# A two-layer hybrid decoder trunk in fp32: q and k by the two-part product, the rotary swap by transfers, the head norm's Newton steps on GpSimd, and attention stages at other distances

## The chip, the cores and the metric

The kernel runs on one core of one Trainium2 chip, in one launch. The core has TensorE (PE in the profile: matrix products and transposes, with PEld for the loading of its stationary operand), VectorE (DVE), ScalarE (ACT), GpSimd (POOL) and SyncE (SP, which here only issues transfers), a scratchpad (SBUF) of 128 partitions, and PSUM, whose 8 banks of 128 x 512 fp32 take PE's results. The metric is the device time in microseconds (us) of one execution; a time shown is the median of several runs.

## The reference

The input x is 256 tokens of width 1024, in fp32. Each of two layers runs a SwiGLU block, a mixer and another SwiGLU block, each followed by a layer norm of `ALPHA*x` plus the block's output. The change lies in the mixer's branch B, differential attention with 8 heads, each with two score maps of dimension 64 and values of width 128:

```
def _mixer(x, ...):
    z = x @ w_in
    u, v, q, k, val, gates = jnp.split(z, SPLITS, axis=-1)
    ...
    q = _rope(q.reshape(bsz, seq, N_DIFF_HEADS, 2, DIFF_HEAD_DIM), cos, sin)
    k = _rope(k.reshape(bsz, seq, N_DIFF_HEADS, 2, DIFF_HEAD_DIM), cos, sin)
    ...
    o = _diff_attention(q, k, val, lam_full)
    o = _rmsnorm(o, diff_ln_g) * (1.0 - lam_init)
    ...
    m = g[:, :, 0] * (h_a @ w_branch[0]) + g[:, :, 1] * (h_b @ w_branch[1])
    return m @ w_out

def _rope(x, cos, sin):
    x1, x2 = jnp.split(xf, 2, axis=-1)
    out = jnp.concatenate([x1 * c - x2 * s, x2 * c + x1 * s], axis=-1)

def _diff_attention(q, k, v, lam):
        s = jnp.where(mask, s, neg)
        p = jax.nn.softmax(s, axis=-1)
        a = p[:, :, 0] - lam * p[:, :, 1]
        return jnp.einsum('bhqk,bkhe->bqhe', a.astype(v.dtype), v)

def _rmsnorm(x, g):
    y = xf * lax.rsqrt(jnp.mean(jnp.square(xf), axis=-1, keepdims=True) + LN_EPS)
```

The mixer's projection `w_in` gives seven sections of width 1024: u, v, q, k, val and two gates.

## The kernel before

**Products in parts.** A matrix product in fp32 is made of three products of a shorter type, fp32r. Each operand is cut into a high part (a copy by ACT, L166 for weights, L173 for activations) and a low part (the difference, a subtraction by DVE, L168 and L174); high times high, low times high and high times low are summed in PSUM. The activations x lie with both parts side by side: `both(k)` (L87) is a 128 x 512 view of the k-th slice of x, the high part of 256 tokens in its first half and the low part in its second; `xh(k)` and `xl(k)` are the halves alone.

**Weights.** They stream from memory in chunks of 1 MB (128 x 2048 fp32). `stream` (L147) issues the load on SP's queue into one of 4 raw buffers, and cuts the chunk in two halves of 1024 columns, each into one of 8 `whi` and 8 `wlo` buffers, so each chunk costs ACT two copies and DVE two subtractions. A weight buffer comes free when PE has used it.

**Two forms of the product that has weights stationary and tokens moving.** One chunk of `pairs` layout holds two blocks of 128 output columns. `gemm_a` (L202, used for q and k) gives both blocks one bank: for each block and each of the 8 slices of x it runs three matmuls with 256 moving columns (`three` with `moving_x`, L200): weight-high with x-high, weight-high with x-low, weight-low with x-high. `gemm_a2` (L212, used for the gates, u, the branch products and the SwiGLU's first products) uses a bank for each block: 8 matmuls of weight-high with 512 moving columns, both parts of x at once (L219), for the two blocks, and then 8 of weight-low with the 256 high columns (L225) for each. What x-low gave lies in the bank's second half. ACT copies it out into `r` (L226), and DVE adds it to the first half into `z` (L227). The buffers `r` come from a pool of four, `s512`, shared with the attention's `pp`.

**Who sets the order.** PE's order is the order of the program, written out by hand: `tc.manual_schedule` covers PE alone. The order of ACT, DVE, POOL and SP is set by the scheduler of the framework, by priorities (`step`, L105, raises the priority number with each chunk) and its own estimate of when things are ready; `issue_after` (`behind`, L143) holds an instruction behind another one. Small pieces of work run between pieces of large products as tasks: a generator that is put beside the products, with a delay, and continued whenever a clock has come far enough. The clock is counted in beats: `gemm_a` beats 1 for each half of a product (L209), `gemm_a2` beats 0.65 for each high half and 0.35 for each low half (L220, L228), so that a product is 2 beats in either form. A `yield n` in a task sets its next piece n beats later.

**The mixer** (L500) runs in this order on PE: the values (`gemm_b2`, L511), the q and k products of four head pairs (L614 to L617), eight in each layer, then eight gate products (L624), v, u with the spatial gating, the branch products and the output product. After each pair's q and k products the attention of that pair is put beside the products that follow, so that it runs during the q and k products of the next pairs and the gate products.

**Rotary** (`rope`, L515). A product's bank holds in each of its 128 partitions one of a head's 128 features (two maps of 64), and in its columns the 256 tokens of each of two heads, the blocks; the two halves of a map's 64 features lie 32 partitions apart. Four copies by ACT (L520), of 32 partitions each, bring the halves into `swap` in exchanged places and scale them; DVE multiplies the bank by the cosine and the scale into `qk` (L524), POOL multiplies `swap` by the signed sine (L526), DVE adds (L527). `swap` comes from a pool of two buffers of 128 x 512 (`t512`, L94), which is shared with the gates' `gz`, the branches' `bz` and the SwiGLU's `silu`.

**Attention of one pair of heads** (`attend`, L530), with delay 3 and these pieces:

1. Scores of the second 128 queries against 256 keys: 4 matmuls (L544) into two side banks. DVE adds the mask and takes the negated maximum of each row (L552, four instructions), ACT takes the exponential and its row sum (L554), DVE forms the reciprocal, the factor with lambda (L558) and the combination of the two maps (L562, two instructions).
2. The same for the first 128 queries, against 128 keys.
3. Transposes of the combined probabilities by PE (L574: four, L579: two), each group copied out of PSUM by ACT (L576, L581).
4. The product with the values (L587, L589) into one side bank. ACT squares it with row sums (L595), into `on`, which is later overwritten. The head's norm is a reciprocal square root: DVE forms the sum with the epsilon (L596, L597), and `rsqrt` (L176) a first guess by integer arithmetic (L180, L181) and three Newton steps of three instructions each on 128 x 4 numbers (L189 to L191), all on DVE. The layer norms use the same function with n = 1, by another path (L186, L187). DVE multiplies the bank by the result into `on` (L599).
5. Transposes of `on` by PE (L605), and the cut in two parts (L610 on ACT, L611 on DVE) into `hb`, the branch product's operand.

PSUM is two pools of four banks: the main one for the large products, the side one for scores, transposes and value products. `gemm_a` holds one main bank for each product; `gemm_a2` holds two.

Of the kernel before, what the change touches and what calls it, by code (L numbers as in the profile page):

```python
# [19 lines left out]
P = 128  # L20
# [30 lines left out]
def trunk(ctx, tc, x, xT, w13a, w13b, w2, wb, wqk, wa, wbr, wo, gateb, sgug, sgub, sguwT, sgubias, lam, diffg,  # L51
# [22 lines left out]
    def bank():  # L74
        return psum.tile([P, 512], F32, tag="main", name=name("bank"))
# [57 lines left out]
    def beside(task, delay):  # L133
        tasks.append([clock[0] + delay, task])
# [3 lines left out]
            for task in list(tasks):  # L138
                turn(task)

    latest = [None, None]

    def behind(ins):  # L143

        return tc.issue_after(ins) if ins is not None else nullcontext()
# [30 lines left out]
    def rsqrt(v, scale, eps, n):  # L176


        ve, y = sm("ve", n), sm("yi", n, I32)
        V.tensor_scalar(out=ve, in0=v, scalar1=scale, scalar2=eps, op0=ALU.mult, op1=ALU.add)  # L180
        V.tensor_scalar(out=y, in0=ve.bitcast(I32), scalar1=-0.5, scalar2=RSQRT_START, op0=ALU.mult, op1=ALU.add)  # L181
        y = y.bitcast(F32)
        for e in (-26 / 27, -8 / 9, -2 / 3):
            a, z = sm("nwa", n), sm("nwy", n)
            if n == 1:
                V.tensor_scalar(out=a, in0=y, scalar1=y, scalar2=ve, op0=ALU.mult, op1=ALU.mult)  # L186
                V.tensor_scalar(out=z, in0=a, scalar1=3.0 * 2.0 ** e, scalar2=y, op0=ALU.subtract, op1=ALU.mult)  # L187
            else:
                V.tensor_tensor(out=a, in0=y, in1=y, op=ALU.mult)  # L189
# [5 lines left out]
    def three(ps, xh, xl, w_hi, w_lo, start, stop, moving_x):  # L195

        order = [(w_hi, xh), (w_hi, xl), (w_lo, xh)] if moving_x else [(w_hi, xh), (w_lo, xh), (w_hi, xl)]
        for n, (w, xx) in enumerate(order):
            l, r = (w, xx) if moving_x else (xx, w)
            PE.matmul(ps, l, r, start=start and n == 0, stop=stop and n == 2)  # L200

    def gemm_a(src, xh, xl):  # L202

        b = bank()
        for n, (hi, lo) in enumerate(stream(src)):
            for k in range(KT):
                s = slice(k * P, (k + 1) * P)
                three(b[:, n * T : (n + 1) * T], xh(k), xl(k), hi[:, s], lo[:, s], k == 0, k == KT - 1, True)
            beat(1)  # L209
        return b  # L210

    def gemm_a2(src, xc, z):  # L212


        b = [bank() for _ in range(2)]
        got = stream(src)
        for n, (hi, lo) in enumerate(got):
            for k in range(KT):
                PE.matmul(b[n], hi[:, k * P : (k + 1) * P], xc(k), start=k == 0, stop=False)  # L219
            beat(0.65)  # L220
        r = s512("r")
        for n, (hi, lo) in enumerate(got):
            s = slice(n * T, (n + 1) * T)
            for k in range(KT):
                PE.matmul(b[n][:, :T], lo[:, k * P : (k + 1) * P], xc(k)[:, :T], start=False, stop=k == KT - 1)  # L225
            A.activation(r[:, s], b[n][:, T:], AF.Copy)  # L226
            V.tensor_tensor(out=z[:, s], in0=b[n][:, :T], in1=r[:, s], op=ALU.add)  # L227
            beat(0.35)  # L228
        return z

    def rows_b(ps, t, k0, piece, xh, xl, kts, c0=0, n=512):

        hi, lo = piece
        for j in range(2):
            k, o = k0 + j, j * 512 + c0
            wh, wl = (w[j][:, c0 : c0 + n] if isinstance(w, list) else w[:, o : o + n] for w in (hi, lo))
            three(ps[:, :n], xh(k)[:, t * P : (t + 1) * P], xl(k)[:, t * P : (t + 1) * P], wh, wl,
                  k == 0, k == kts - 1, False)
        beat(n / 1024)

    def gemm_b(src, kts, xh, xl, done, tail=4, last=()):
# [258 lines left out]
    def mixer(l, i, norm):  # L500
# [11 lines left out]

        hb = slots("hb", 2 * KT, F32R)

        def rope(ps, scale):  # L515

            sw = t512("swap")
            for q in range(4):
                o, i = q * 32, (q ^ 1) * 32
                A.activation(sw[o : o + 32, :], ps[i : i + 32, :], AF.Copy, scale=scale)  # L520
            z = slots("qk", 2)[0]
            z3, s3 = z.rearrange("p (j t) -> p j t", j=2), sw.rearrange("p (j t) -> p j t", j=2)
# [3 lines left out]
            G.tensor_tensor(out=s3, in0=s3, in1=s, op=ALU.mult)  # L526
            V.tensor_tensor(out=z, in0=z, in1=sw, op=ALU.add)  # L527
            return z

        def attend(hp, qT, kT):  # L530
# [33 lines left out]
                return pp[0]  # L564

            second = exps(1)
            yield 1
            first = exps(0)
            yield 2
            b = side_bank()  # L570
            for j in range(2):
                for c in range(2):
# [6 lines left out]
                PE.transpose(b[:, j * P : (j + 1) * P], first[:, j * P : (j + 1) * P], ident)  # L579
# [19 lines left out]
            V.tensor_tensor(out=on.rearrange("p (q e) -> p q e", q=4), in0=b.rearrange("p (q e) -> p q e", q=4),  # L599
                             in1=r.unsqueeze(2).to_broadcast([P, 4, P]), op=ALU.mult)  # L600
            yield 3
            b = side_bank()
            for j in range(2):
                for t in range(NT):
# [186 lines left out]
```

## Time and profile before

| | |
|---|---|
| Time, median of 3 runs | 1251.56 us (1251.5 to 1252.19) |
| The profiled execution's own time | 1251.36 us |
| Its span in the trace | 1249.6 us |
| Granted TensorE clock, mean | 0.998 |
| Data moved by transfers | 237.69 MB, mean 190 GB/s |
| HBM read and written | 235.47 MB and 1.05 MB |

In the profile, the first part gives the busy time of each engine with its share of the span. The second cuts the span in 40 slices, with a digit for tenths busy:

```profile
DVE  6777567788587887765687665677886878866654
ACT  6776456897565566663466664468875555766530
POOL 0100000210000000000000000001200000000000
...
DMA  9954555445665547555547545554456654565530
```

The mixers' attention stages are where POOL has its few digits: slices 8 and 9 of layer 0, and 28 and 29 of layer 1. The list of costly groups is read as line, engine, operation, output from inputs (partitions x elements), then busy time, the mean of one in ns, and the idle time of that engine just before with what ended it:

```profile
L168 DVE TENSOR_TENSOR wlo<-raw,whi 128x1024 fp32r<-128x1024 f32 (+1 forms) x442 | 490.2, 1122 | 153.5 <-ACT whi L166 80.1
...
L219 PE MATMUL bank<-x,whi 128*128 128x512 f32 x1536 | 369.4, 392 | 0.0
...
L225 PE MATMUL bank<-x,wlo 128*128 128x256 f32 x1536 | 200.7, 284 | 0.0
```

The duration of one matmul there is its pipelined length; what it costs PE's stream is read from the chain of waits, where a number of them in sequence stand with their time together. The same chain, taken in order of time, names the line and the number of instructions of each piece of PE's work; a list of the waits of an engine names what it waited for, how long, how often, and the longest. The timeline gives single instructions or runs of one line with start and length.

### The profile page before, as it was taken

Reading aid. Unit: us, or ns where it says so; the run is one execution under the profiler, and the core shown is the slowest. Engines: PE = TensorE matmul, PEld = TensorE weight load, DVE = VectorE, ACT = ScalarE, POOL = GpSimd, SP = SyncE. Lnnn points to the kernel's source line nnn. Section 1 sums busy time; section 2 is a strip of 40 time slices with the busy share of each in tenths; the row PEclk is TensorE's granted clock in tenths of the full one; section 3 lists DMA queues with packets and bytes.
Section 4 is the critical chain, followed back from the end, with each engine's and each line's share of the span. In section 5 each row is a group of like instructions: output and inputs, shape, how many; then the busy total and the mean of one; then the engine's idle time right before and its main releaser. Section 6 shows DMA issues by size and latency. Waiting matters only on the chain.

```text
span 1249.6 us, 18211 instructions
## 1 busy us (share of the span) xinstructions
PE 1236.8 (99%) x6951; PEld 1077.1 (86%) x6951; DVE 899.9 (72%) x1637; ACT 764.1 (61%) x1365; POOL 43.8 (4%) x62
## 2 busy tenths in 40 slices
PE   9999999999999999999999999999999999999997
PEld 8888888988888888888888888899888888888886
DVE  6777567788587887765687665677886878866654
ACT  6776456897565566663466664468875555766530
POOL 0100000210000000000000000001200000000000
PEclk9999999999999999999999999999999999999999
DMA  9954555445665547555547545554456654565530
GB/s 355 318 198 175 186 182 193 175 142 185 209 215 183 187 152 249 187 186 186 201 165 241 193 163 190 196 202 136 153 185 209 216 181 169 201 235 177 180 118 34
DMA packets 37608, 237.69 MB, mean 190 GB/s; under 512 B 4321, under 2 KB 5393, under 8 KB 11409
## 3 DMA queue, kind: packets, MB, share of 16 engines
q1 hardware_dynamic: 33552, 223.89, 51.3%
q0 software_dynamic: 3536, 12.13, 2.9%
q8 instruction: 54, 0.88, 0.3%
q10 hardware_dynamic: 432, 0.52, 0.1%
q14 instruction: 34, 0.27, 0.1%
HBM read 235.47 MB, written 1.05 MB: 189 GB/s over the span
## 4 chain that ended last, share of the span: by engine, by line
PE 98%; DVE 1%; ACT 1%; issue 0%; DVEq 0%
PE bank L200 43%; PE bank L219 33%; PE bank L225 17%; PE bank L315 2%; PE sbank L544 1%; PE sbank L435 1%; PE sbank L664 1%; PE sbank L589 0%; PE sbank L327 0%; ACT swap L520 0%; PE sbank L605 0%; PE sbank L469 0%; DVE pp L562 0%; ACT pp L554 0%; PE sbank L587 0%; PE sbank L574 0%
## 5 line engine op out<-in xcount | busy, mean ns | idle before, releaser
L168 DVE TENSOR_TENSOR wlo<-raw,whi 128x1024 fp32r<-128x1024 f32 (+1 forms) x442 | 490.2, 1122 | 153.5 <-ACT whi L166 80.1
L166 ACT ACTIVATE whi<-raw 128x1024 fp32r<-128x1024 f32 (+1 forms) x442 | 425.9, 978 | 278.9 <-PE bank L200 145.6
L219 PE MATMUL bank<-x,whi 128*128 128x512 f32 x1536 | 369.4, 392 | 0.0
L219 PEld LDWEIGHTS bank<-x,whi 128*128 128x128 f32 x1536 | 282.3, 188 | 54.9
L225 PEld LDWEIGHTS bank<-x,wlo 128*128 128x128 f32 x1536 | 196.2, 191 | 7.3 <-issue 0.7
L225 PE MATMUL bank<-x,wlo 128*128 128x256 f32 x1536 | 200.7, 284 | 0.0
L200 PE MATMUL bank<-whi,hhi 128*128 128x512 f32 (+1 forms) x374 | 141.4, 378 | 0.0
L200 PE MATMUL bank<-wlo,hhi 128*128 128x512 f32 (+1 forms) x374 | 141.1, 377 | 0.0
L200 PE MATMUL bank<-whi,hlo 128*128 128x512 f32 (+1 forms) x374 | 141.0, 377 | 0.0
L226 ACT ACTIVATE r<-bank 128x256 f32<-128x256 f32 x224 | 83.3, 378 | 53.6 <-PE bank L225 53.2
L200 PE MATMUL bank<-whi,x 128*128 128x512 f32 x328 | 106.5, 394 | 0.0
L200 PE MATMUL bank<-x,whi 128*128 128x256 f32 x512 | 94.4, 286 | 0.0
L200 PEld LDWEIGHTS bank<-x,whi 128*128 128x128 f32 x512 | 79.8, 192 | 2.6 <-issue 2.0
L200 PEld LDWEIGHTS bank<-whi,hlo 128*128 128x128 f32 x374 | 70.4, 188 | 12.9
L200 PEld LDWEIGHTS bank<-wlo,hhi 128*128 128x128 f32 x374 | 70.4, 188 | 12.8
L200 PEld LDWEIGHTS bank<-whi,hhi 128*128 128x128 f32 x374 | 70.4, 188 | 12.7
L200 PE MATMUL bank<-x,wlo 128*128 128x256 f32 x256 | 72.5, 283 | 0.0
L200 PEld LDWEIGHTS bank<-whi,x 128*128 128x128 f32 x328 | 61.6, 188 | 12.5
L174 DVE TENSOR_TENSOR hlo<-silu,hhi 128x256 fp32r<-128x256 f32 x72 | 30.6, 425 | 52.5 <-ACT hhi L173 52.5
L200 PE MATMUL bank<-wlo,x 128*128 128x512 f32 x164 | 64.0, 390 | 0.0
L441 ACT ACTIVATE xf<-sbank,ln_b,ln_g 128x128 f32<-128x128 f32 x80 | 30.1, 456 | 40.1 <-PE sbank L435 40.1
L227 DVE TENSOR_TENSOR silu<-bank,r 128x256 f32<-128x256 f32 x144 | 54.3, 417 | 0.1
(166 smaller groups left out, 1348.4 us busy)
## 6 DMA issues: line engine op xcount, KB each, us to landing
raw<-in_w13a SPq DMA_DIRECT2D x72, 1024.0 KB, 5.1
raw<-in_w SPq DMA_DIRECT2D x40, 1024.0 KB, 4.8
raw<-in_wa SPq DMA_DIRECT2D x24, 1024.0 KB, 4.9
raw<-in_wb SPq DMA_DIRECT2D x16, 1024.0 KB, 5.1
raw<-in_wqk SPq DMA_DIRECT2D x16, 1024.0 KB, 5.6
raw<-in_wbr SPq DMA_DIRECT2D x16, 1024.0 KB, 5.0
raw<-in_w13b SPq DMA_DIRECT2D x12, 1024.0 KB, 5.0
raw<-in_wo SPq DMA_DIRECT2D x8, 1024.0 KB, 4.9
```

The source lines that it names most:

```text
L166: A.activation(h, r, AF.Copy)
L168: V.tensor_tensor(out=w, in0=r, in1=h.bitcast(F32), op=ALU.subtract)
L174: return a.ins, V.tensor_tensor(out=lo, in0=src, in1=hi.bitcast(F32), op=ALU.subtract).ins
L200: PE.matmul(ps, l, r, start=start and n == 0, stop=stop and n == 2)
L219: PE.matmul(b[n], hi[:, k * P : (k + 1) * P], xc(k), start=k == 0, stop=False)
L225: PE.matmul(b[n][:, :T], lo[:, k * P : (k + 1) * P], xc(k)[:, :T], start=False, stop=k == KT - 1)
L226: A.activation(r[:, s], b[n][:, T:], AF.Copy)
L227: V.tensor_tensor(out=z[:, s], in0=b[n][:, :T], in1=r[:, s], op=ALU.add)
L315: PE.matmul(ps[t][m], x[:, j, o + t * P : o + (t + 1) * P], y, start=k0 + j == 0 and o == 0 and y is hi, stop=k0 + j == KT - 1 and y is lo)
L435: PE.transpose(b[:, k * P : (k + 1) * P], self.y[t][:, h * 512 + k * P : h * 512 + (k + 1) * P], ident)
L441: A.activation(xf[:, s], b[:, s], AF.Identity, scale=self.gT[:, f], bias=self.bT[:, f])
L544: PE.matmul(banks[m][:, j * nk : (j + 1) * nk], rows(qT, m, j, t * P, P), rows(kT, m, j, 0, nk), start=True, stop=True)
```

## The change

**Products.** `gemm_a` is gone; q and k go through `gemm_a2` with the weights as before. It takes a scale (for q, 1/8; for k, 1) and the buffer for `r`, here from `t512`, the pool of two that `swap` uses too; with a scale other than 1 DVE's add becomes a multiply-add.

**Swap.** `rope` now starts from `z` in SBUF, not from the bank. Four transfers from SBUF to SBUF, issued on SP's queue, take the place of ACT's four copies. DVE multiplies `z` by the cosine in place, POOL and DVE go on as before.

**Newton steps.** For n > 1, which is the head norm alone, the three Newton steps run on POOL, each in four instructions instead of three. The guess stays on DVE.

**After the value product.** ACT first copies the bank to `on`, squares inside PSUM, and, 3.9 beats later, scales `on` in place with four instructions, each held behind the last evacuation that `gemm_a2` has put on ACT at that place of the program (`emptied`). DVE's multiply by the norm is gone.

**Stages.** The first delay goes from 3 to 3.9 beats; the distances between the pieces go from 1, 2, 3, 3 to 0.6, 2.6, 2.3, and then 3.9 to the scaling and 0.9 from there to the final transposes.

```diff
-                V.tensor_tensor(out=a, in0=y, in1=y, op=ALU.mult)
-                V.tensor_tensor(out=a, in0=a, in1=ve, op=ALU.mult)
-                V.scalar_tensor_tensor(out=z, in0=a, scalar=3.0 * 2.0 ** e, in1=y, op0=ALU.subtract, op1=ALU.mult)
+                G.tensor_tensor(out=a, in0=y, in1=y, op=ALU.mult)
+                G.tensor_tensor(out=a, in0=a, in1=ve, op=ALU.mult)
+                G.tensor_scalar(out=a, in0=a, scalar1=3.0 * 2.0 ** e, scalar2=None, op0=ALU.subtract)
+                G.tensor_tensor(out=z, in0=a, in1=y, op=ALU.mult)
...
-    def gemm_a(src, xh, xl):
...
-    def gemm_a2(src, xc, z):
+    def gemm_a2(src, xc, z, scale=1.0, r=None):
...
-        r = s512("r")
+        r = s512("r") if r is None else r
...
-            A.activation(r[:, s], b[n][:, T:], AF.Copy)
-            V.tensor_tensor(out=z[:, s], in0=b[n][:, :T], in1=r[:, s], op=ALU.add)
+            emptied[0] = A.activation(r[:, s], b[n][:, T:], AF.Copy, scale=scale).ins
+            if scale == 1.0:
+                V.tensor_tensor(out=z[:, s], in0=b[n][:, :T], in1=r[:, s], op=ALU.add)
+            else:
+                V.scalar_tensor_tensor(out=z[:, s], in0=b[n][:, :T], scalar=scale, in1=r[:, s], op0=ALU.mult,
+                                       op1=ALU.add)
...
-        def rope(ps, scale):
+        def rope(src, scale):
+            z = gemm_a2(src, both, slots("qk", 2)[0], scale, t512("r"))
             sw = t512("swap")
             for q in range(4):
                 o, i = q * 32, (q ^ 1) * 32
-                A.activation(sw[o : o + 32, :], ps[i : i + 32, :], AF.Copy, scale=scale)
-            z = slots("qk", 2)[0]
+                nc.sync.dma_start(sw[o : o + 32, :], z[i : i + 32, :])
...
-            V.scalar_tensor_tensor(out=z3, in0=ps.rearrange("p (j t) -> p j t", j=2), scalar=scale, in1=c,
-                                   op0=ALU.mult, op1=ALU.mult)
+            V.tensor_tensor(out=z3, in0=z3, in1=c, op=ALU.mult)
             G.tensor_tensor(out=s3, in0=s3, in1=s, op=ALU.mult)
             V.tensor_tensor(out=z, in0=z, in1=sw, op=ALU.add)
...
             second = exps(1)
-            yield 1
+            yield 0.6
             first = exps(0)
-            yield 2
+            yield 2.6
...
-            yield 3
+            yield 2.3
...
             on = slots("on", 2)[0]
+            A.activation(on, b, AF.Copy)
             ss, s2 = sm("ss", 4), sm("s2", 4)
             for q in range(4):
                 s = slice(q * P, (q + 1) * P)
-                A.activation(on[:, s], b[:, s], AF.Square, accum_out=ss[:, q : q + 1])
+                A.activation(b[:, s], b[:, s], AF.Square, accum_out=ss[:, q : q + 1])
...
-            V.tensor_tensor(out=on.rearrange("p (q e) -> p q e", q=4), in0=b.rearrange("p (q e) -> p q e", q=4),
-                             in1=r.unsqueeze(2).to_broadcast([P, 4, P]), op=ALU.mult)
-            yield 3
+            yield 3.9
+            for q in range(4):
+                s = slice(q * P, (q + 1) * P)
+                with behind(emptied[0]):
+                    A.activation(on[:, s], on[:, s], AF.Copy, scale=r[:, q : q + 1])
+            yield 0.9
...
         for hp in range(HEADS // 2):
-            qT = rope(gemm_a(wqk[l, hp, 0], xh, xl), HD ** -0.5)
-            kT = rope(gemm_a(wqk[l, hp, 1], xh, xl), 1.0)
-            beside(attend(hp, qT, kT), 3)
+            qT = rope(wqk[l, hp, 0], HD ** -0.5)
+            kT = rope(wqk[l, hp, 1], 1.0)
+            beside(attend(hp, qT, kT), 3.9)
```

The parameter `moving_x` of `three` goes too, since no product uses it any more.

More of the change, by code (lines that the diff above doesn't have):

```diff
@@ L139, in finish_tasks @@
                 turn(task)
-    latest = [None, None]
+    latest, emptied = [None, None], [None]
     def behind(ins):
@@ L188, in rsqrt, with three @@
             else:
-                V.tensor_tensor(out=a, in0=y, in1=y, op=ALU.mult)
-                V.tensor_tensor(out=a, in0=a, in1=ve, op=ALU.mult)
-                V.scalar_tensor_tensor(out=z, in0=a, scalar=3.0 * 2.0 ** e, in1=y, op0=ALU.subtract, op1=ALU.mult)
+                G.tensor_tensor(out=a, in0=y, in1=y, op=ALU.mult)
+                G.tensor_tensor(out=a, in0=a, in1=ve, op=ALU.mult)
+                G.tensor_scalar(out=a, in0=a, scalar1=3.0 * 2.0 ** e, scalar2=None, op0=ALU.subtract)
+                G.tensor_tensor(out=z, in0=a, in1=y, op=ALU.mult)
             y = z
         return y
[L195 to L200, printed above, removed]
-    def gemm_a(src, xh, xl):
[L204 to L210, printed above, removed]
-    def gemm_a2(src, xc, z):
+    def three(ps, xh, xl, w_hi, w_lo, start, stop):
+        for n, (w, xx) in enumerate([(w_hi, xh), (w_lo, xh), (w_hi, xl)]):
+            PE.matmul(ps, xx, w, start=start and n == 0, stop=stop and n == 2)
+    def gemm_a2(src, xc, z, scale=1.0, r=None):
         b = [bank() for _ in range(2)]
@@ L237, in rows_b @@
             three(ps[:, :n], xh(k)[:, t * P : (t + 1) * P], xl(k)[:, t * P : (t + 1) * P], wh, wl,
-                  k == 0, k == kts - 1, False)
+                  k == 0, k == kts - 1)
         beat(n / 1024)
@@ L519, in rope @@
                 o, i = q * 32, (q ^ 1) * 32
-                A.activation(sw[o : o + 32, :], ps[i : i + 32, :], AF.Copy, scale=scale)
-            z = slots("qk", 2)[0]
-            z3, s3 = z.rearrange("p (j t) -> p j t", j=2), sw.rearrange("p (j t) -> p j t", j=2)
+                nc.sync.dma_start(sw[o : o + 32, :], z[i : i + 32, :])
+            z3, s3 = (v.rearrange("p (j t) -> p j t", j=2) for v in (z, sw))
             c, s = (v.unsqueeze(1).to_broadcast([P, 2, T]) for v in (cos_t, sin_t))
-            V.scalar_tensor_tensor(out=z3, in0=ps.rearrange("p (j t) -> p j t", j=2), scalar=scale, in1=c,
-                                   op0=ALU.mult, op1=ALU.mult)
+            V.tensor_tensor(out=z3, in0=z3, in1=c, op=ALU.mult)
             G.tensor_tensor(out=s3, in0=s3, in1=s, op=ALU.mult)
```

## Prediction

> **What bounds the kernel now.** I read the page's busy shares and its chain of waits first, then the list of what TensorE (PE) waited for, then windows over the stage that the change touches.
>
> ```profile
> PE 1236.8 (99%) x6951; PEld 1077.1 (86%) x6951; DVE 899.9 (72%) x1637; ACT 764.1 (61%) x1365; POOL 43.8 (4%) x62
> ...
> PE 98%; DVE 1%; ACT 1%; issue 0%; DVEq 0%
> ```
> ```profile
> PE sbank L579 <- DVE pp L562: 1.8, 2, 0.9
> ...
> PE sbank L544 <- DVE mx L552: 0.9, 2, 0.4
> ```
> ```profile
> 211.96:322.62 110.66, 109.33 (x793) 100.16 (x791) 89.18 (x225) 90.20 (x208) 14.53 (x14) 1.00 0.52 177
> 830.06:940.72 110.66, 109.33 (x793) 100.15 (x792) 89.20 (x225) 90.20 (x208) 14.56 (x14) 1.00 0.53 177
> ```
>
> PE is the chain. Its order is written out by hand, so the time falls only if PE has less to do or waits less. Inside the kernel it waits 2.7 us in all, 0.9 + 0.4 us in each layer, on DVE. The windows run from the first q/k product to the last gate product of each layer: columns are length, busy time of PE, PEld, DVE, ACT, POOL, then clock, DMA share and GB/s. The two layers agree to 0.02 us, and DVE and ACT are 81% busy there, so a late step of either has little time to catch up. The clock is 1.00 throughout.
>
> What PE pays for each piece, from the chain in order of time:
>
> ```profile
> 55.92 3.65 PE bank L219 x16
> 59.57 1.91 PE bank L225 x16
> ...
> 224.88 7.20 PE bank L200 x60
> 232.08 1.06 PE sbank L544 x8
> ...
> 236.21 0.65 PE sbank L544 x8
> ...
> 242.81 0.44 PE sbank L574 x4
> 243.25 0.22 PE sbank L579 x2
> ...
> 254.19 0.22 PE sbank L587 x2
> ...
> 255.53 2.87 PE bank L200 x24
> ```
>
> The second stall of a layer looks like this in the timeline (GpSimd is POOL):
>
> ```profile
> 274.91 1.63 DVE L562 SCALAR_TENSOR_TENSOR pp<-pp,c,pp 128x128 f32<-128x128 f32 x2
> ...
> 275.12 1.29 POOL L526 TENSOR_TENSOR swap<-swap,sin_t 128x512 f32<-128x512 f32 x1 [9.23 <-ACT swap L520]
> ...
> 276.60 0.33 PE L579 MATMUL sbank<-ident,pp 128*128 128x128 f32 x1 [0.89 <-DVE pp L562]
> ```
>
> DVE finishes pair 2's probabilities late, and PE stands before their transposes. That is where I look for the next stall.
>
> **The change, part by part.**
>
> *Products.* A q or k product is 48 matmuls of 256 columns at 7.20/60 = 0.120 us: 5.76 us. In the other form it is 3.65 + 1.91 = 5.56 us. That is 0.20 us less for each of 16: **-3.2 us**, all on PE's chain. The same form already runs at that pace for the gates, so little is open here: bounds -2.9 and -3.2.
>
> *The old stalls.* The stages stand elsewhere, so the **-2.7 us** of waits go; whether others come is the main question below.
>
> *The swap.* Four copies on ACT go; two evacuations on ACT and one more on DVE each come. Four transfers of 64 KB on SP take their place.
>
> ```profile
> 2.19 0.91 SPq L299 DMA_DIRECT2D raw<-in_w13b  x2
> ```
> ```profile
> raw<-in_wqk SPq DMA_DIRECT2D x16, 1024.0 KB, 5.6
> ...
> out_x<-xtok SPq DMA_DIRECT2D x2, 128.0 KB, 2.0
> ```
>
> SP needs 0.45 us for each issue, 1.8 us for four. The trace has no SBUF-to-SBUF transfer; its landing is bounded below by the 2.0 us of the quiet store and above by the 5.6 us of a weight load in traffic. I take 2.5, nearer the store in size. Then: evacuations 0.8, issues 1.8, landing 2.0 to 5.6, the multiply on POOL 1.3 to 2.05, the add 0.6: 6.5 to 10.9 us after the product. The scores that need it now stand four gemm halves later, 2 x 5.56 = 11.1 us. That cover hides it; without it each late microsecond is PE's. SP now issues all eight q/k loads before the first swap, and each later load waits behind a swap, by up to one product (5.6 us). Those loads are used three products later (16.7 us) and land in 5.6: no cost. `r` and `swap` share two buffers, so the evacuation of product n waits on ACT for the add of product n-2: also 11.1 us behind it, covered likewise, and ACT's splits are what queues there.
>
> *Newton steps on GpSimd.* In the built order POOL has, in this sequence, the multiply for pair 2's k, twelve Newton steps of pair 0, then the multiply for pair 3's q. DVE has `yi` of pair 0, a split, z*cos, one evacuation, and then the add that needs that last multiply. So DVE stands at the add until Newton is through, and behind it stand the second evacuation, pair 2's row maxima and combinations, which PE's third transposes need. What it costs needs these rows:
>
> ```profile
> 211.56 5.76 DVE L168 TENSOR_TENSOR wlo<-raw,whi 128x1024 fp32r<-128x1024 f32 x5
> ...
> 222.49 0.69 DVE L527 TENSOR_TENSOR qk<-qk,swap 128x512 f32<-128x512 f32 x1 [0.69 <-POOL swap L526]
> 223.10 2.58 DVE L168 TENSOR_TENSOR wlo<-raw,whi 128x1024 fp32r<-128x1024 f32 x2
> ...
> 234.60 0.42 DVE L552 CUSTOM_DVE_ANT_0 pp<-sbank,mask 128x256 f32<-128x256 f32 x1
> ...
> 235.97 1.22 DVE L168 TENSOR_TENSOR wlo<-raw,whi 128x1024 fp32r<-128x1024 f32 x1
> ...
> 237.79 0.87 DVE L562 SCALAR_TENSOR_TENSOR pp<-pp,c,pp 128x256 f32<-128x256 f32 x2
> ...
> 256.09 0.61 DVE L562 SCALAR_TENSOR_TENSOR pp<-pp,c,pp 128x128 f32<-128x128 f32 x2
> ...
> 261.13 0.16 DVE L189 TENSOR_TENSOR nwa<-yi 128x4 f32<-128x4 f32 x1
> ...
> 262.90 0.69 DVE L599 TENSOR_TENSOR on<-sbank,nwy 128x512 f32<-128x512 f32 x1
> ...
> 263.51 1.22 DVE L168 TENSOR_TENSOR wlo<-raw,whi 128x1024 fp32r<-128x1024 f32 x1
> ...
> 263.83 2.05 POOL L526 TENSOR_TENSOR swap<-swap,sin_t 128x512 f32<-128x512 f32 x1 [5.08 <-ACT swap L520]
> ...
> 299.95 0.75 DVE L227 TENSOR_TENSOR gz<-bank,r 128x256 f32<-128x256 f32 x2
> ```
> ```profile
> 1.42 0.20 POOL masks.py:29 MEMSET mask<- 128x128 f32 x1
> 1.69 0.29 POOL masks.py:30 TENSOR_SCALAR_AFFINE_SELECT mask<-mask 128x128 f32<-128x128 f32 x1
> ```
>
> From start to start on DVE: a split 1.14 ((5.76-1.22)/4), a 512-wide pass 0.61, an evacuation 0.33, the four 256-wide row maxima 1.37 (234.60 to 235.97), the four of 128 some 0.84 (0.34 each less 0.13, since a split of 1024 columns and a pass of 512 differ by 0.53, which is 0.13 per 128), two combinations 0.87 or 0.61, a small step 0.20 (nine from 261.13 to 262.90).
>
> From pair 1's second transposes to pair 2's, DVE's built order holds five splits 5.7, four passes 2.4, three evacuations 1.0, row maxima 2.2, combinations 1.5, eight small steps 1.6: 14.4 us. PE does the same stretch in 1.91 + 1.06 + 3.65 + 0.65 + 1.91 + 1.34 (value product, 254.19 to 255.53) + 3.65 + 0.44 (final transposes, priced as the first) + 0.44 + 0.22 = 15.3 us. That leaves DVE 0.9 us for waits, and it has two.
>
> First the add. A Newton step on POOL is not in the trace. Below it stands DVE's 0.20; above, a 128x128 select with the 0.07 us between the end of a memset (1.62) and the dependent select (1.69): 0.36. I take 0.27, the memset with that gap: 3.2 us for twelve. The first step also has to wait for the split beside it: at 263.83 POOL's multiply took 2.05 instead of 1.29 because DVE's split ran until 264.73. The multiply adds 1.36. DVE itself arrives 1.14 + 0.61 + 0.33 = 2.1 us after `yi`. So it waits 2.4 + 1.36 - 2.1 = 1.7 at the least, 3.2 + 1.1 + 0.6 (one pass let through) + 1.36 - 2.1 = 4.2 at the most with this step; I take 3.4.
>
> The Trainium skill's page GPSIMD Engine Reference, section Specifications, says that GpSimd's access to SBUF is shared with VectorE and contends with VectorE instructions that have two SBUF inputs. The trace agrees (2.05 against 1.29 us). By that rule each of the twelve steps could meet a split, 12 x 1.14 = 13.7 us; DVE's standing still at the add ends it earlier, so the sum keeps the row.
>
> Second, the square of the row sums, which waits for pair 2's last exponentials on ACT:
>
> ```profile
> L166 ACT ACTIVATE whi<-raw 128x1024 fp32r<-128x1024 f32 x360 | 378.2, 1059 | 218.6 <-PE bank L219 108.0 <-PE bank L200 100.1 <-issue 7.4
> ...
> L554 ACT ACTIVATE pp<-pp,mx 128x256 f32<-128x256 f32 x32 | 15.9, 499 | 10.6 <-DVE mx L552 10.5
> ...
> L554 ACT ACTIVATE pp<-pp,mx 128x128 f32<-128x128 f32 x32 | 12.5, 391 | 0.2
> ```
>
> ACT does four exponentials (2.0 us, half of them behind the maxima), a split, two short ones, a split, two short ones: 1.0 + 2 x 1.06 + 4 x 0.39 = 4.7 us after the last 256-wide maximum; DVE is there after 3.2 (a split 1.14, small steps 0.4, maxima 0.84, combinations 0.87). Wait 1.5 us, or 0 if ACT's splits run earlier.
>
> 14.4 + 3.4 + 1.5 - 15.3 = 4.0 us late. In the stretch before, DVE holds 13.4 us of steps and 1 to 2 us of waits against PE's 14.8, so it enters level: 0.3 us late, between 0.2 early and 1.5 late. **New stall: 4.3 us per layer, 8.6 in all**; bounds 0.6 (14.4 + 1.7 + 0 - 15.3 - 0.2) and 6.3 (14.4 + 4.2 + 1.5 - 15.3 + 1.5). It falls on PE at pair 0's final transposes or pair 2's transposes, whichever is reached first.
>
> Copying `on`, squaring into PSUM and scaling on ACT cost ACT some 2 us per pair, and it gives up 1.6 us for each product: off the chain.
>
> **Sum.** The profiled execution took 1251.36 us, 0.2 below the median shown, 1249.6 of it span. 1251.36 - 3.2 - 2.7 + 8.6 = **1254.1 us**.
>
> **Rivals.**
>
> *No new stall.* If the swap lands in 2 us, Newton steps take 0.2 and ACT's splits lie earlier, DVE keeps up: 1251.36 - 5.9 = 1245.5 us. For it: ACT is relieved of 2.35 - 0.76 = 1.6 us per product, if a copy there is taken at the 0.59 us that four need:
>
> ```profile
> L520 ACT ACTIVATE swap<-bank 32x512 f32<-32x512 f32 x64 | 37.7, 588 | 1.1
> ...
> L226 ACT ACTIVATE r<-bank 128x256 f32<-128x256 f32 x224 | 83.3, 378 | 53.6 <-PE bank L225 53.2
> ```
> Against it: 14.4 of 15.3 us is already spoken for.
>
> *Swaps queue behind weight loads.* z*cos rewrites what the transfers read, so DVE stands at it until they land. Pair 2's q swap is issued after two 1 MB loads; at 5.6 us each they are not through. If it and its neighbours land at the upper bound, DVE is 3.1 us later at each of two adds before pair 1's transposes, and half of that is not caught up: 3.5 us more per layer, 1254.1 + 7 = 1261 us. Against it: the loads start some 7 us before that swap. The Trainium skill's page DMA: Bandwidth & Descriptors, section Queues, rings and completion order, says that each DMA engine takes a queue's descriptors in order; by that the swap would stand behind both loads. No run here shows it yet.
>
> *The products do not get faster*, because short stages now cut into longer matmuls: 1254.1 + 3.2 = 1257.3. The gates' rows speak against it.
>
> **How the numbers follow.** Forecast 0.56, no new stall 0.29, late swaps 0.12, products no faster 0.03. A measurement of this kernel can tell about 0.2%, 2.5 us, from no change. The forecast's own range, with the stall at 2.5 to 6.3 us per layer, is 1250.5 to 1258; it gives faster 0.04, same 0.20, slower 0.32. No new stall gives faster 0.28, same 0.01; the other two slower 0.15. Together faster 0.32, same 0.21, slower 0.47. For 8 in 10 the range must reach both signs: 1245 to 1260.5.
>
> **What would show it.** Right: PE's waits in the changed profile name pair 2's transposes or pair 0's final ones, 3 to 5 us once per layer, with DVE idle before the rope's add (releaser POOL); matmuls of q and k in rows of 3.65 and 1.91. Wrong: PE's waits stay under 1 us per layer (then DVE's steps or POOL's Newton were overpriced), or DVE idles mainly before z*cos with a DMA as releaser (late swaps), or PE waits before scores (the 11.1 us cover was not enough).

## The result, and the profile after

| | before | after |
|---|---|---|
| Time, median | 1251.57 us (1251.19 to 1252.21, 19 runs) | 1253.9 us (1253.03 to 1254.47, 19 runs) |
| Ratio to before, 95% interval | | 1.0018 [1.0012, 1.0024] |
| The profiled execution's own time and span | 1251.36, 1249.6 us | 1253.48, 1251.8 us |

The change made the kernel slower by 0.18%; the forecast was 1254.1 us. In the changed kernel the lines stand some eight lower: the swap's transfers are L514, z*cos L517, POOL's multiply L518, the add L519, the scores L536, row maxima L544, exponentials L546, combinations L554, the transposes of probabilities L566 and L571, the value product L579 and L581, the square of the row sums L589, ACT's scaling L596, the final transposes L601; a product's matmuls are L208 and L214.

The page's busy times, and then what PE waited for (total, times, longest):

```profile
PE 1237.1 (99%) x6695; PEld 1062.7 (85%) x6695; DVE 896.3 (72%) x1589; ACT 749.1 (60%) x1373; POOL 78.9 (6%) x158
```
```profile
PE sbank L601 <- ACT on L596: 3.3, 4, 1.4
...
PE sbank L579 <- DVE mx L544: 0.7, 2, 0.4
PE sbank L536 <- ACT aT L568: 0.5, 1, 0.5
```

The old waits (transposes and scores, 2.7 us) are gone, and 4.5 us of others stand in their place, most of it at the final transposes, for ACT's scaling. PE's busy time is 0.3 us above that of before, though its products are shorter: matmuls that run long count as busy, and some do, as will be seen.

The stages from the first q product to the first product behind the gates, in the windows' columns of before:

```profile
211.49:323.73 112.24, 110.19 (x666) 93.86 (x665) 87.77 (x200) 82.65 (x212) 31.89 (x62) 0.98 0.58 193
830.99:942.87 111.88, 109.37 (x665) 93.01 (x664) 86.86 (x200) 82.61 (x212) 31.40 (x62) 1.00 0.59 194
```

In the kernel before, the same stretch of layer 0 runs from 211.76 us to 322.62, so 110.86 us (the prediction's window begins 0.20 us into it); in layer 1 it is 110.85. So layer 0 is 1.4 us longer and layer 1 is 1.0, 2.4 in all, where the span grew by 2.2. Layer 0's clock in the first row is 0.98.

Around the longest wait, the timeline of POOL, DVE and ACT in layer 0 (start, length, engine, line; in brackets the idle time before and what ended it):

```profile
262.60 1.23 DVE L168 TENSOR_TENSOR wlo<-raw,whi 128x1024 fp32r<-128x1024 f32 x1
...
262.73 1.16 POOL L189 TENSOR_TENSOR nwa<-yi 128x4 f32<-128x4 f32 x1 [5.44 <-DVE yi L181]
...
264.55 0.69 DVE L517 TENSOR_TENSOR qk<-qk,cos_t 128x512 f32<-128x512 f32 x1 [0.73 <-DMA swap<-qk]
...
265.16 0.42 DVE L217 TENSOR_TENSOR qk<-bank,r 128x256 f32<-128x256 f32 x1
265.38 0.20 POOL L189 TENSOR_TENSOR nwa<-nwy 128x4 f32<-128x4 f32 x1
...
267.55 1.28 POOL L518 TENSOR_TENSOR swap<-swap,sin_t 128x512 f32<-128x512 f32 x1
268.86 0.69 DVE L519 TENSOR_TENSOR qk<-qk,swap 128x512 f32<-128x512 f32 x1 [3.28 <-POOL swap L518]
...
270.26 0.51 ACT L546 ACTIVATE pp<-pp,mx 128x256 f32<-128x256 f32 x1 [6.40 <-DVE mx L544]
...
274.06 1.29 POOL L518 TENSOR_TENSOR swap<-swap,sin_t 128x512 f32<-128x512 f32 x1 [5.23 <-DVE pp L554]
...
274.21 1.16 DVE L589 TENSOR_TENSOR s<-sums 128x4 f32<-128x4 f32 x1
...
275.95 1.27 ACT L596 ACTIVATE on<-on,nwy 128x128 f32<-128x128 f32 x4
```

It reads from the top: POOL takes up pair 0's Newton steps at 262.73, reaches the multiply for pair 3's q at 267.55, and DVE stands 3.28 us at the add. So pair 2's maxima and exponentials are late (ACT stands 6.40 us before them), and ACT, which has pair 0's scaling behind those exponentials, comes to it at 275.95. And on PE:

```profile
273.02 2.00 PE L208 MATMUL bank<-x,whi 128*128 128x512 f32 x8
276.39 0.33 PE L601 MATMUL sbank<-ident,on 128*128 128x128 f32 x1 [1.37 <-ACT on L596]
276.98 0.62 PE L601 MATMUL sbank<-ident,on 128*128 128x128 f32 x3 [0.26 <-ACT on L596]
277.35 3.65 PE L208 MATMUL bank<-x,whi 128*128 128x512 f32 x8
...
292.47 2.01 PE L208 MATMUL bank<-x,whi 128*128 128x512 f32 x8
...
294.67 2.10 PE L208 MATMUL bank<-x,whi 128*128 128x512 f32 x8
```

From the eight matmuls to the product behind the transposes it is 4.33 us in the first group (277.35 - 273.02) and 2.20 in the undisturbed second: 2.1 us lost. Then the next eight take 3.65 us for 2.10: 1.5 us more, with nothing waited for. The windows of that stretch and of the same one in layer 1 say why (the clock stands behind POOL's time):

```profile
277.27:280.68 3.41, 3.41 (x11) 2.66 (x10) 3.05 (x9) 3.38 (x13) 0.00 (x0) 0.53 0.17 26
...
896.85:900.30 3.45, 3.45 (x24) 3.00 (x23) 2.91 (x10) 3.42 (x13) 0.00 (x0) 1.00 0.22 31
```

For 3.4 us the granted clock was about half, in layer 0 alone, although both layers have the same wait of 1.37 us before it.

### The profile page after: what moved, and what is told of

Read it like the earlier page. It is cut to its first block, busy times and chain, and to the rows that moved or that the text cites. A ratio compares the mean times of both kernels' runs of the same rounds, so it can differ in the third digit from the quotient of the medians.

```text
span 1251.8 us, 17887 instructions
## 1 busy us (share of the span) xinstructions
PE 1237.1 (99%) x6695; PEld 1062.7 (85%) x6695; DVE 896.3 (72%) x1589; ACT 749.1 (60%) x1373; POOL 78.9 (6%) x158
## 5 line engine op out<-in xcount | busy, mean ns | idle before, releaser
L208 PE MATMUL bank<-x,whi 128*128 128x512 f32 x1792 | 434.9, 393 | 0.0
L208 PEld LDWEIGHTS bank<-x,whi 128*128 128x128 f32 x1792 | 329.5, 189 | 67.5 <-issue 2.7
L214 PEld LDWEIGHTS bank<-x,wlo 128*128 128x128 f32 x1792 | 229.3, 191 | 7.8
L214 PE MATMUL bank<-x,wlo 128*128 128x256 f32 x1792 | 235.3, 283 | 0.0
L215 ACT ACTIVATE r<-bank 128x256 f32<-128x256 f32 x256 | 95.9, 377 | 58.5 <-PE bank L214 58.0
L518 POOL TENSOR_TENSOR swap<-swap,sin_t 128x512 f32<-128x512 f32 x16 | 24.5, 1532 | 413.9 <-DVE wlo L168 186.0
L386 DVE SCALAR_TENSOR_TENSOR xtok<-xtok,bank 128x512 f32<-128x512 f32 (+1 forms) x25 | 16.5, 661 | 42.3 <-PE bank L199 42.3
L546 ACT ACTIVATE pp<-pp,mx 128x256 f32<-128x256 f32 (+1 forms) x64 | 28.3, 443 | 24.3 <-DVE mx L544 24.3
```

Source lines behind the costliest of these rows:

```text
L215: emptied[0] = A.activation(r[:, s], b[n][:, T:], AF.Copy, scale=scale).ins
L386: V.scalar_tensor_tensor(out=self.y[t][:, s], in0=self.y[t][:, s], scalar=self.scale, in1=ps, op0=ALU.mult, op1=ALU.add)
L546: A.activation(p[:, s], p[:, s], AF.Exp, bias=mx[:, a], scale=-1.0, accum_out=sums[:, a])
```

## The experiments

Each kernel ran 4 to 11 times beside the kernel before, whose median was 1251.67, 1251.52 and 1251.81 us in the three groups (four, four and four rows of the table).

| kernel | median, us | ratio to before, 95% interval |
|---|---|---|
| newton_dve | 1250.99 | 0.9995 [0.9986, 1.0004] |
| newton_more | 1256.69 | 1.0040 [1.0026, 1.0054] |
| scale_early | 1254.05 | 1.0018 [1.0010, 1.0027] |
| swap_act | 1268.25 | 1.0138 [1.0124, 1.0152] |
| mul_dve | 1245.34 | 0.9949 [0.9938, 0.9961] |
| newton_dve_early | 1250.89 | 0.9994 [0.9986, 1.0003] |
| old_stages | 1262.23 | 1.0084 [1.0071, 1.0097] |
| prod_swap | 1257.64 | 1.0044 [1.0032, 1.0057] |
| mul_q3 | 1248.92 | 0.9976 [0.9967, 0.9985] |
| mul_pair3 | 1247.64 | 0.9965 [0.9953, 0.9978] |
| both_dve | 1245.12 | 0.9946 [0.9934, 0.9959] |
| before_mul | 1248.15 | 0.9971 [0.9960, 0.9983] |

**newton_dve.** The three Newton steps on DVE again.

```diff
-                G.tensor_tensor(out=a, in0=y, in1=y, op=ALU.mult)
-                G.tensor_tensor(out=a, in0=a, in1=ve, op=ALU.mult)
-                G.tensor_scalar(out=a, in0=a, scalar1=3.0 * 2.0 ** e, scalar2=None, op0=ALU.subtract)
-                G.tensor_tensor(out=z, in0=a, in1=y, op=ALU.mult)
+                V.tensor_tensor(out=a, in0=y, in1=y, op=ALU.mult)
+                V.tensor_tensor(out=a, in0=a, in1=ve, op=ALU.mult)
+                V.scalar_tensor_tensor(out=z, in0=a, scalar=3.0 * 2.0 ** e, in1=y, op0=ALU.subtract, op1=ALU.mult)
```

> The Newton steps of the head norm go back to DVE (three instructions each); the rest is the changed kernel. Theory (DVE stands at pair 3's add because POOL does pair 0's Newton steps first, and pair 2's maxima, exponentials, ACT's scaling and PE's final transposes of pair 0 are late behind it): nine steps of 0.2 us on DVE replace a wait of 3.3 us in layer 0 and 2.2 us in layer 1, and fill the wait for the swap's landing before them; the add comes some 1.8 us earlier, PE's wait at pair 0's final transposes (2.1 us lost per layer) falls to 0.5 or less, and no half clock follows it: 1248 to 1250.5 us. Rival A (the scaling is late only because it stands behind pair 2's exponentials on ACT): DVE has 1.8 us more work per pair, nothing gained, 1253 to 1256. Rival B (the swap transfers land late): unchanged, 1253 to 1254.5.

Measured 1250.99, just above the theory's range; both rivals are out. Its waits of PE and of DVE's add:

```profile
PE sbank L600 <- ACT on L595: 1.7, 4, 0.6
```
```profile
DVE qk L518 <- POOL swap L517: 4.5, 5, 1.2
```

No half clock follows. But PE still waits, and DVE still stands 4.5 us at adds, with no Newton step on POOL. So the Newton steps are not all of it.

**newton_more.** The first two multiplies of each step are done twice on POOL.

```diff
+                G.tensor_tensor(out=a, in0=y, in1=y, op=ALU.mult)
+                G.tensor_tensor(out=a, in0=a, in1=ve, op=ALU.mult)
                 G.tensor_tensor(out=a, in0=y, in1=y, op=ALU.mult)
```

> Each Newton step on POOL does its first two multiplies twice (18 instructions for 12, the same result). Theory: six more at 0.28 us keep POOL 1.7 us longer ahead of the multiply of pair 3's q; DVE's wait at the add grows from 3.3 and 2.2 to about 5 and 3.9 us, and PE pays it in each layer: 2.5 to 4 us more, 1256.5 to 1258. Rivals A and B: POOL has time to spare, 1253.5 to 1254.5.

Measured 1256.69, as the theory says: 2.8 us more than the changed kernel for 3.4 us of steps (twice six at 0.28), with the longest wait at the add up from 3.3 to 4.7:

```profile
DVE qk L521 <- POOL swap L520: 11.3, 5, 4.7
```

**scale_early.** ACT's scaling ahead of pair 2's exponentials.

```diff
-            yield 3.9
+            yield 2.2
...
-            yield 0.9
+            yield 2.6
```

> ACT's scaling of pair 0 is put 2.2 beats behind the value product, ahead of pair 2's exponentials in ACT's order; the final transposes stay where they are. Rival A: the loss at pair 0's final transposes goes (2.1 us per layer) and with it the half clock of layer 0 (1.5 us): about 1248. Theory: DVE is as late as before, so PE waits next at pair 2's transposes for the combinations (L554), 1.5 to 2.7 us per layer: 1251.5 to 1254.

Measured 1254.05, just above the theory's range. The final transposes wait no more, and PE stands at pair 2's transposes instead, for the combinations, as the theory has it:

```profile
PE sbank L571 <- DVE pp L554: 3.7, 2, 1.9
```

**newton_dve_early.** Both edits, newton_dve and scale_early.

> The Newton steps on DVE and the scaling 2.2 beats behind the value product, ahead of pair 2's exponentials on ACT. With the Newton steps done early, ACT does not wait at the scaling. Theory: the 1.4 us per layer that the final transposes of pair 0 still cost go, but most of it comes back at pair 2's transposes, since DVE is done with them only 0.2 us before PE now: 1249.5 to 1251. Rival A (the scaling's place is the rest of the stall): 1248 to 1249.3.

Measured 1250.89, in the theory's range and no gain over newton_dve. The place of the scaling decides where PE waits, not how long.

**swap_act.** ACT's copies from `z` in place of the transfers.

```diff
-                nc.sync.dma_start(sw[o : o + 32, :], z[i : i + 32, :])
+                A.activation(sw[o : o + 32, :], z[i : i + 32, :], AF.Copy)
```

> The four transfers of each swap become four copies by ACT from the same tile. Rival B: without the landing (2 to 4.6 us) the multiply and the add come earlier, and most of the new stalls go: 1247 to 1250. Theory: POOL's Newton steps still stand ahead of pair 3's multiply; ACT has some 2 us more per product: 1252.5 to 1256.

Measured 1268.25: both were wrong, and the transfers are the better form by 14 us here. By estimate up to 5 us of that is clock: this trace has four stretches of 3.4 us at half clock, the changed kernel's has one. ACT now stands 20.2 us in all before its copies, until DVE has made `z`, and what follows them in its order is late too. DVE multiplies `z` by the cosine in place, so it must wait for the copies, and POOL's multiply is later still:

```profile
DVE qk L519 <- POOL swap L518: 18.3, 14, 2.5
DVE qk L517 <- ACT swap L514: 11.8, 12, 1.5
```

**old_stages.** The changed kernel with the distances of before.

```diff
-            beside(attend(hp, qT, kT), 3.9)
+            beside(attend(hp, qT, kT), 3)
```

with the yields 1, 2, 3, 2.1 and 0.9.

> The changed kernel with the distances of before (delay 3; 1, 2, 3; the scaling 2.1 beats behind the value product and the final transposes 0.9 behind it). Theory: the scores come 0.9 beats (2.5 us) earlier, 8.6 us behind the last product instead of 11.1, so the swap, the multiply and the add no longer lie under cover; PE waits before scores or the value product too: 1255 to 1262. Rival D (the new distances make the stall): 1248 to 1252.

Measured 1262.23, just above the theory's range. PE waits at the scores for the add, at transposes, and at the final ones (3.5 us):

```profile
PE sbank L571 <- DVE pp L554: 4.8, 4, 1.6
...
PE sbank L536 <- DVE qk L519: 2.9, 4, 1.3
```

So the changed kernel needs the new distances. Only the 2.9 us at the scores name the swap's add; that the rest comes from the shorter cover too is not shown.

**prod_swap.** The kernel before with `gemm_a2` and the transfers, as in the change, and nothing else of it.

> The kernel before with only the products in the other form and the swap by transfers; Newton steps, head norm and distances as before. Theory: 3.2 us less on PE's chain and no Newton steps on POOL, but DVE has the second evacuation and a cover of 8.3 us for swap and add: 1249 to 1255, with PE's waits at scores or at the transposes of the probabilities. If the products alone carry the gain and nothing is late: 1246 to 1248.5.

Measured 1257.64 (1254.47 to 1260.36), above the range, at the places named: 5.8 us at the scores, 5.4 at transposes. The spread goes with the granted clock, 0.998 in the fastest run and 0.995 in the slowest.

**mul_dve.** The multiply by the sine on DVE.

```diff
-            G.tensor_tensor(out=s3, in0=s3, in1=s, op=ALU.mult)
+            V.tensor_tensor(out=s3, in0=s3, in1=s, op=ALU.mult)
```

> The rotary's multiply by the sine goes from POOL to DVE; the Newton steps stay on POOL, where nothing that DVE needs stands behind them now. Theory (the stall is DVE's wait for POOL): the waits at the add go (3.3 and 2.2 us, and some 1.3 us elsewhere) against 0.6 us more work on DVE for each product, 1.2 us in the stretch that decides; PE's loss falls from 4.0 us per layer to 1 to 2.5: 1247.5 to 1250.5 us. Rival C (DVE is late by its own work, 14.4 of 15.3 us, and the waits only fill gaps): 1.2 us more work per stretch makes it later, 1255 to 1257.

Measured 1245.34, below the range: 8.6 us under the changed kernel, and 0.5% faster than before. Rival C is out. PE's list of waits holds one entry, the start's:

```profile
PE sbank L320 <- DVE warm L316: 1.0, 1, 1.0
```

Why more than the waits at the add came back is seen in DVE's groups, of the changed kernel first (busy time, mean ns, idle before):

```profile
L517 DVE TENSOR_TENSOR qk<-qk,cos_t 128x512 f32<-128x512 f32 x16 | 13.5, 846 | 2.4 <-DMA swap<-qk 2.4
L519 DVE TENSOR_TENSOR qk<-qk,swap 128x512 f32<-128x512 f32 x16 | 10.9, 684 | 8.6 <-POOL swap L518 8.3
L554 DVE SCALAR_TENSOR_TENSOR pp<-pp,c,pp 128x256 f32<-128x256 f32 x16 | 8.0, 539 | 0.2
L589 DVE TENSOR_TENSOR s<-sums 128x4 f32<-128x4 f32 x8 | 5.3, 662 | 0.0
```

and of mul_dve:

```profile
L519 DVE TENSOR_TENSOR qk<-qk,swap 128x512 f32<-128x512 f32 x16 | 10.9, 684 | 0.1
L517 DVE TENSOR_TENSOR qk<-qk,cos_t 128x512 f32<-128x512 f32 x16 | 10.9, 684 | 0.2 <-DMA swap<-qk 0.2
L518 DVE TENSOR_TENSOR swap<-swap,sin_t 128x512 f32<-128x512 f32 x16 | 10.9, 683 | 0.0
L554 DVE SCALAR_TENSOR_TENSOR pp<-pp,c,pp 128x256 f32<-128x256 f32 x16 | 7.0, 480 | 0.1
...
L589 DVE TENSOR_TENSOR s<-sums 128x4 f32<-128x4 f32 x8 | 1.2, 153 | 0.3 <-ACT pp L546 0.2
```

An instruction of four elements a partition took 662 ns in the mean, and 1.16 us beside POOL's multiply, where it takes 153 when POOL multiplies nothing. With POOL's multiplies DVE loses 2.6 us at L517, 1.0 at L554 and 4.1 at L589, which run longer, and 8.5 in idle time at the add L519: 16.2 us, to be spared sixteen multiplies that cost it 10.9. (L517's own idle time, 2.2 us more, names the swap's landing and not POOL.) Part of the 8.5 us is the queue of Newton steps ahead of the multiply. In mul_dve the Newton steps stayed on POOL, and harm nothing. Nor does the landing make the stall: mul_dve's swaps land in 3.2 us in the median, and PE waits for none.

**mul_q3 and mul_pair3.** Only some multiplies on DVE: that of pair 3's q, or those of its q and k.

```diff
+            E.tensor_tensor(out=s3, in0=s3, in1=s, op=ALU.mult)
...
+            qT = rope(wqk[l, hp, 0], HD ** -0.5, V if hp == 3 else G)
```

> Of the eight multiplies by the sine of a layer only one goes from POOL to DVE: that of pair 3's q, which stands behind the Newton steps of pair 0. Theory (the stall comes from that one place): the add waits no more for POOL, and comes some 2.3 us earlier in layer 0 and 1.2 us in layer 1, where the landing of the swap holds it; the loss at the value product and at the final transposes of pair 0 and the half clock go, some 4 us in layer 0 and 1.5 to 2 in layer 1: 1247.5 to 1249.5. Rival E (each POOL multiply holds DVE up through the SBUF that both read, and the eight add up): one in eight gives an eighth of the gain of 8.6 us, about 1252.8.

> The multiplies of pair 3's q and k go to DVE, the other six of a layer stay on POOL. Theory: k's multiply on POOL no longer stretches the square of pair 2's row sums (1.16 us where the same instruction takes 0.15 elsewhere): 1 to 2 us less than with q's alone, 1245.5 to 1248. Rival E: a quarter of the gain, about 1251.8.

Measured 1248.92 and 1247.64, both in the theory's ranges. Of the 8.6 us by the medians, the one multiply behind the Newton steps carries some 5.0, pair 3's k another 1.3, and the other six of a layer 2.3. (The 5.0 holds the half clock of layer 0, which mul_q3's trace does not have, and the shares compare groups whose kernel before differs by 0.3 us.) So the place dominates and rival E, an equal share for each multiply, is out; but the others on POOL cost 3.6 us too.

**both_dve.** Multiplies and Newton steps on DVE.

> All eight multiplies of a layer and the Newton steps on DVE; POOL has neither. If the Newton steps on POOL are worth something once nothing waits behind them, DVE is 1.8 us per pair longer, with 14.4 + 1.2 + 1.8 = 17.4 us of steps in a stretch of 15.3 (less what lies idle elsewhere): 1248 to 1252. If POOL's share was the only harm: 1245 to 1246.5.

Measured 1245.12, the same as mul_dve. DVE had room for all of it; in the window between pair 1's and pair 2's transposes:

```profile
261.50:277.25 15.75, 15.75 (x105) 13.37 (x104) 15.23 (x55) 12.40 (x42) 1.09 (x2) 1.00 0.59 187
```

PE runs through, and DVE is busy 15.23 of 15.75 us. Both versions beat both kernels; with the multiplies on DVE, it makes no difference that can be measured where the Newton steps run.

**before_mul.** The kernel before with the one edit of mul_dve.

> The kernel before with the multiply by the sine on DVE and nothing else. If POOL's multiply is what DVE was late for there too, its 2.7 us of waits shrink: 1249 to 1251. If DVE had no room there: 1252 to 1256.

Measured 1248.15: 3.7 us faster, beyond the expectation. The groups of the combinations, before and then in before_mul:

```profile
L562 DVE SCALAR_TENSOR_TENSOR pp<-pp,c,pp 128x128 f32<-128x128 f32 x16 | 9.0, 606 | 0.3
```
```profile
L562 DVE SCALAR_TENSOR_TENSOR pp<-pp,c,pp 128x128 f32<-128x128 f32 x16 | 4.9, 348 | 0.2
```

PE's waits at transposes and scores are gone from its list. So the old stalls, too, were DVE held up by POOL's multiply: beside it at the combinations, and behind it at the add at 265.91 us, which waited 0.59 us for it just ahead of the row maxima that the scores need.

## Why the prediction came out right, point by point

- *Products, -3.2 us.* Held. Without any stall, the stretch of layer 0 is 107.54 us in mul_dve (107.55 in layer 1), and 1251.36 - 3.2 - 2.7 = 1245.5 against 1245.34 measured in mul_dve.

```profile
212.21:319.75 107.54, 107.54 (x665) 92.77 (x664) 86.95 (x208) 82.60 (x212) 21.27 (x54) 1.00 0.59 202
```

- *The old stalls, -2.7 us.* They went, and were a little larger: 110.86 - 8 x 0.20 - 107.54 = 1.7 us per layer for 1.35. Their cause was misread. The prediction quoted the two combinations at 1.63 us and POOL's multiply in the rows next to each other, and took it as "DVE finishes pair 2's probabilities late"; the pair takes 0.61 without the multiply beside it. The prediction priced POOL held by a split, but put the other direction, DVE held by POOL's multiply, at nothing.
- *The swap.* The median landing was 2.0 us (2.5 was taken), an issue 0.60 us (0.45 was taken), and the cover of 11.1 us held: PE never waits at scores for the swap. Late swaps cost DVE 2.4 us in all at L517, as the rival said in kind, not in size.
- *Newton steps.* Sized well: twelve steps and the split beside the first took 4.82 us (262.73 to 267.55) for 4.9 at the most, 0.28 us a step for 0.27, and the wait at the add was 3.28 us in layer 0 for 3.4. It was 2.15 in layer 1, where DVE had stood 1.67 us at z*cos for the landing first.
- *The square of the row sums, 1.5 us for ACT's exponentials.* This step failed in its reason. It did not wait for ACT at all (the square reads only the first map's sums, which are done two short exponentials earlier); it was stretched by 1.0 us (1.16 for 0.15) by POOL's multiply. The size was near by chance.
- *DVE's 14.4 of 15.3 us.* Too full. In mul_dve the stretch took PE 15.76 us, and DVE was busy in 14.89 of it with two multiplies of 0.68 inside it, so some 13.5 without them. DVE's own work left 2.2 us, not 0.9. The window of mul_dve between the two transposes:

```profile
261.55:277.31 15.76, 15.76 (x104) 13.36 (x103) 14.89 (x45) 12.76 (x43) 5.44 (x12) 1.00 0.50 165
```

- *New stall, 4.3 us per layer.* 112.24 - 107.54 = 4.7 and, in layer 1, 111.88 - 107.55 = 4.3 us. At pair 0's final transposes, the place named, PE lost 2.1 us in each layer; the list has 1.6 of it as waits, where the prediction's sign was 3 to 5. The rest lies where the prediction had none, by the starts of PE's instructions against mul_dve's: 0.9 us in each layer before, at a value product and at transposes of probabilities, and behind it 1.6 us in layer 0 at the half clock and 1.2 in layer 1 at pair 3's scores. That the too-full DVE, the unseen holds and the unforeseen clock add up so near to the forecast is luck.

The sum by these sizes is -3.2 - 3.4 + 9.0 = +2.4 us in the stretches, where the prediction had +2.7. The queue, the total and the place of half of the stall were right; how the harm is shared between the Newton steps and the multiplies was not: putting the Newton steps back gives 2.9 us, moving the multiplies 8.6. An order of POOL with the Newton steps behind the multiply of pair 3's q was not run, so it is open whether the order alone would do.

## What to carry to other kernels

An elementwise operation given to GpSimd was not free for VectorE: here sixteen of them, some behind Newton steps, cost VectorE 16.2 us in waits and stretched instructions, against 10.9 for doing them itself. Where an instruction takes two or three times its usual time just before a stall, look at what ran beside it before calling its engine late. And work added to an in-order queue is priced by what already stands behind it: the same Newton steps cost nothing once no multiply followed them there.

## What the runs showed of the hardware that was not expected

*VectorE and GpSimd hold each other up, and the one that starts second waits.* A step of four elements on POOL took 1.16 us beside a split, and a square of four elements on DVE 1.16 us beside POOL's multiply. Each ended with the instruction that had started before it: at 263.89 us with the split at 263.83, and at 275.37 with POOL's multiply at 275.35. A long one that starts second does its own work after that, as here in the changed kernel:

```profile
227.82 2.01 POOL L518 TENSOR_TENSOR swap<-swap,sin_t 128x512 f32<-128x512 f32 x1 [3.06 <-DMA swap<-qk]
...
229.26 1.66 DVE L168 TENSOR_TENSOR wlo<-raw,whi 128x1024 fp32r<-128x1024 f32 x1
```

POOL's multiply took 2.01 us for 1.29, behind a split that had started at 227.46, and the next split took 1.66 for 1.22 behind the multiply. DVE's evacuation at 265.16 in the timeline above, which reads one operand from PSUM, kept its 0.42 us, and POOL's step beside it its 0.20. So did z*cos in the kernel before, which read the bank: 0.69 us beside POOL's multiply at 247.72. In the changed kernel z*cos reads `z` from SBUF and takes 0.85 us in the mean, 0.68 where POOL multiplies nothing: moving the rotary off the bank exposed it, and the prediction did not price that. The Trainium skill's page GPSIMD Engine Reference, section Specifications, names contention with VectorE instructions that have two SBUF inputs; the trace agrees in the cases shown here.

*PE's clock halves after short waits, by where they fall.* A wait of 1.37 us was followed by 3.4 us at a clock near 0.5 in one layer and by none in the other. In every trace of this case the half clock inside the run begins a whole number of steps of 3.413 us after the clock first became full (80 in the changed kernel). Counted in these steps, the one before the half clock of layer 0, and the two at the same wait in layer 1, are:

```profile
274.07:277.48 3.41, 1.78 (x10) 1.00 (x9) 3.41 (x8) 3.41 (x11) 1.28 (x1) 1.00 0.65 274
...
891.89:895.30 3.41, 2.62 (x15) 1.94 (x13) 3.41 (x16) 3.41 (x11) 1.29 (x1) 1.00 0.77 240
895.30:898.71 3.41, 2.57 (x12) 1.96 (x13) 3.41 (x8) 3.38 (x14) 0.00 (x0) 1.00 0.25 106
```

In layer 0 all of the idle time lies in one step, 1.63 us of it; in layer 1 a step ends inside the wait, and each has 0.8. Every half clock inside these traces follows a step with 1.63 us idle or more. One step of newton_more with 1.78 us idle was followed by none, so the idle time alone does not decide. The Trainium skill's page TensorE: Matmul & The Clock Gate, section HAM oscillation — how this bites in real kernels, gives the rule as no idle gaps of PE over some 3.4 us; here gaps of 1.37 and 0.26 us in one step were enough once. By what its first part says of a window that runs freely, the place of the wait in that window would decide; the two layers agree with that.
